# TensorE's order in a two-layer hybrid trunk: one stream at fixed rates, or threads and a rough engine model

## The chip, the cores and the metric

The kernel runs on one core of one Trainium2 chip. The metric is the device time of one execution in microseconds (us); less is better. TensorE (PE in the profile) does the matmuls, VectorE (DVE), ScalarE (ACT) and GpSimd (POOL) the elementwise work, and SyncE (SP) issues the DMA transfers. PEld is TensorE's loading of weights, which runs beside its matmuls.

## The reference

One inference step of a backbone of two layers. 128 context tokens and 512 latent tokens (640 in all) of width 1024 go through the same weights. Each layer normalises and modulates its input, projects it, and gives the columns to three mixers in parallel: A, grouped attention; B, attention over a compressed latent; C, a recurrence over the tokens in both directions. Their outputs are gated, merged and projected.

```python
def _context_mixer(h, lp):
    a_q, a_k, a_v, a_z, b_q, b_ckv, b_kr, b_z, c_in, c_z, gates = _split_in(h @ lp['w_in'])
    q, k, v = _a_qkv(a_q, a_k, a_v, lp)
    ya = _block_attention(q.reshape(...), k, v) * jax.nn.silu(a_z)
    ...
    yb = _mla_attend(qb, ckv, b_kr, lp) * jax.nn.silu(b_z)
    yc, s_f, s_b = _branch_c(c_in, s0, s0, lp)
    yc = yc.astype(h.dtype) * jax.nn.silu(c_z)
    return _merge(gates, ya, yb, yc, lp), k, v, ckv, b_kr, s_f, s_b

# the recurrence of mixer C, for each of 8 heads and both directions
def step(state, inp):
    r_t, w_t, k_t, v_t, a_t, b_t = inp
    sa = jnp.einsum('bhij,bhj->bhi', state, a_t)
    state = (state * w_t[:, :, None, :] + sa[..., None] * b_t[:, :, None, :]
             + v_t[..., None] * k_t[:, :, None, :])
    y_t = jnp.einsum('bhij,bhj->bhi', state, r_t)
    return state, y_t
```

The latent tokens run the same mixers, with rotary positions, and see the cached context as well.

## The kernel before

Activations lie with features on the 128 partitions and the 640 tokens along the row, split into a high and a low part (`hh`, `hl`); each product of full accuracy is three matmuls, high x high, low x high, high x low (L225 to L227 in `proj_half`, L178 to L180 in `mm3`). A tile of 128 output columns is a "unit": `load_w1` brings its weights in two halves (tile `wraw`), ACT casts each to `whi` (L174), DVE or POOL subtracts to get `wlo` (L175), and `proj_half` makes two times 24 matmuls of 320 columns into the PSUM tile `pcm`. Two weight buffers alternate.

Each layer has the stages scan (mixer C, with most projections beside it), attention (mixers A and B), merge and output projection. Only scan and attention are touched.

In the scan stage the heads go in four pairs, p = 0 to 3. For each, `c_prep` makes the decays and the factors `L1` and `BK` (L549 and L551 on DVE, L553 and L554 on POOL), `c_pairs` makes chunk products (`pA`, L613) and transposes, `c_inverse` inverts a triangular matrix by 30 pairs of dependent DVE products (L660, L662) and some small matmuls (`px`, `py`), `c_values` transposes the values. `c_scan` then goes through 2 context and 8 latent chunks, both directions at a time. Each of its 10 steps is a chain over engines: matmul `sca` (L767), copies to `wbd` (L769, L770), matmul `scb` (L773), copies to `VZ` (L775, L776) and, on POOL, to `ubd` (L778), matmul `scb` (L782), matmul `sca` on `ubd` (L786), and the new state on DVE (L799). `c_gn` normalises a pair's output: a chain over POOL, DVE and ACT (L811 to L835), transposes `pyt` (L840), and the last products.

What lies beside a scan is one generator, `self.stream` (the functions `period`, `prepare`, `keys`, `fillers` in `run`): the preparation of the next pair, then units in a fixed order and number from the table `PLAN` (`share`, `fb`, `at`). `pump` takes pieces of it at a fixed rate, three times in each scan step; what is left when the scan ends is run by `drain`. Then come `c_values` of the next pair and `c_gn` of the one that ended. In attention, `stream(i)` holds the next pair's keys and queries, and `head` pumps it at the rates of `PLAN`; `head` makes four tiles of scores (`sc`, L955), each followed by its maximum (L958) and exponential (`P`, L960), then five times transposes (`pp`, L970), the split into `ph` and `pl` (L163, L164), and the two products `po` (L974, L975).

This order of writing is a preference alone: the framework's scheduler then orders the instructions of every engine, TensorE's too, by an own simulation of times, and takes among those that are ready the one written first. On the chip each engine then runs its list in that order.

## Time and profile before

| what | value |
|---|---|
| median of 3 runs | 2347.88 us (2346.89 to 2358.01) |
| the profiled execution's own time | 2358.59 us |
| its span, first to last instruction | 2356.9 us |
| mean granted clock of TensorE | 0.934 |
| busy: PE, PEld | 2144.3 us (91%), 2025.6 us (86%) |
| busy: DVE, ACT, POOL | 1603.2 us (68%), 1107.0 us (47%), 694.8 us (29%) |
| matmuls | 15380 |
| DMA | 209.70 MB, 89 GB/s |

The rows of the trace further below are of the profiled execution. The granted clock is a mean over a stretch: 1.00 is TensorE at 2.4 GHz, 0.50 at 1.2 GHz. A matmul's busy time overlaps that of the next one.

### The profile page before, as it was taken

The numbers are of one execution on the slowest core, as the hardware profiler recorded it, in microseconds if no ns is written. First come the engines' busy times: TensorE is split into PE (matmuls) and PEld (weight loads), VectorE is DVE, ScalarE is ACT, GpSimd is POOL, SyncE is SP. The second block draws the span as 40 slices with busy tenths as digits, with TensorE's granted clock in tenths as the row PEclk, the third lists the DMA queues.
The fourth block names the chain that finished last, engine by engine and source line by source line (L and its number), as shares of the span: only waits on it lengthen the run. The fifth ranks groups of instructions, "written<-read, shape, count | busy, mean of one in ns | idle before, by whom it ended". The sixth has DMA issues, their size and how long they took to land. (4 is left out here: it accounts for less than half of the span.)

```text
span 2356.9 us, 40407 instructions
## 1 busy us (share of the span) xinstructions
PE 2144.3 (91%) x15380; PEld 2025.6 (86%) x15380; DVE 1603.2 (68%) x3054; ACT 1107.0 (47%) x2462; POOL 694.8 (29%) x769
## 2 busy tenths in 40 slices
PE   8889998999779889999989999999897888999998
PEld 6889998989678777879988999989896877788898
DVE  4667878868544677775748778687774458677673
ACT  4544443444343567662344444443442436677333
POOL 3332536145233311102033143351632341210021
PEclk9999998999789899999989999999996989999999
DMA  6232222222223311125622322222222220110552
GB/s 224 77 100 80 82 75 81 86 90 94 79 75 98 107 36 52 39 76 172 203 64 68 106 73 86 74 71 84 81 82 76 73 95 30 51 46 17 186 183 89
DMA packets 111762, 209.70 MB, mean 89 GB/s; under 512 B 14416, under 2 KB 33488, under 8 KB 111568
## 3 DMA queue, kind: packets, MB, share of 16 engines
q1 hardware_dynamic: 111568, 207.12, 27.6%
q8 instruction: 121, 1.98, 0.3%
q14 instruction: 73, 0.60, 0.1%
HBM read 163.52 MB, written 43.55 MB: 88 GB/s over the span
## 5 line engine op out<-in xcount | busy, mean ns | idle before, releaser
L225 PE MATMUL pcm<-hh,whi 128*128 128x320 f32 x1952 | 636.1, 326 | 16.5 <-ACT xv L378 2.9
L227 PE MATMUL pcm<-hh,wlo 128*128 128x320 f32 x1952 | 627.9, 322 | 11.3 <-DVE wlo L175 11.3
L226 PE MATMUL pcm<-hl,whi 128*128 128x320 f32 x1952 | 625.1, 320 | 0.0
L225 PEld LDWEIGHTS pcm<-hh,whi 128*128 128x128 f32 x1952 | 382.1, 196 | 24.5 <-DVE modc L252 5.0
L227 PEld LDWEIGHTS pcm<-hh,wlo 128*128 128x128 f32 x1952 | 380.9, 195 | 15.1 <-DVE wlo L175 13.9
L226 PEld LDWEIGHTS pcm<-hl,whi 128*128 128x128 f32 x1952 | 381.9, 196 | 1.2
L174 ACT CAST whi<-wraw 128x512 fp32r<-128x512 f32 (+1 forms) x356 | 226.9, 666 | 322.0 <-PE pcm L226 116.8
L175 DVE TENSOR_TENSOR wlo<-wraw,whi 128x512 fp32r<-128x512 f32 (+1 forms) x262 | 220.9, 857 | 78.3 <-ACT whi L174 74.9
L175 POOL TENSOR_TENSOR wlo<-wraw,whi 128x512 fp32r<-128x512 f32 x94 | 124.4, 1337 | 157.4 <-ACT whi L174 152.4
L778 POOL COPY ubd<-VZ 64x128 f32<-64x128 f32 x160 | 65.0, 406 | 354.9 <-ACT VZ L775 324.3
L164 DVE TENSOR_TENSOR pl<-pp,ph 128x512 fp32r<-128x512 f32 x160 | 107.9, 684 | 35.5 <-ACT ph L163 34.7
L958 DVE TENSOR_REDUCE nm<-sc 128x1 f32<-128x640 f32 x128 | 104.2, 818 | 28.7 <-PE sc L955 27.5
L178 PE MATMUL pm<-yh,whi 128*128 128x320 f32 x384 | 121.5, 317 | 2.0 <-DVE OT L992 1.5
L179 PE MATMUL pm<-yl,whi 128*128 128x320 f32 x384 | 121.1, 315 | 0.5 <-DVE yl L167 0.4
L180 PE MATMUL pm<-yh,wlo 128*128 128x320 f32 x384 | 120.8, 315 | 0.7 <-DVE wlo L175 0.7
L163 ACT CAST ph<-pp 128x512 fp32r<-128x512 f32 x160 | 92.1, 585 | 46.5 <-PE pp L970 36.6
L960 ACT ACTIVATE P<-sc,nm 128x640 f32<-128x640 f32 x128 | 101.9, 797 | 17.4 <-DVE nm L958 14.0
L970 PE MATMUL pp<-small,P 128*128 128x128 f32 x640 | 102.0, 284 | 7.3 <-DVE pl L164 2.5
L767 PE MATMUL sca<-VZ,L 128*128 128x64 f32 x640 | 96.5, 296 | 11.1 <-DVE VZ L799 11.1
L767 PEld LDWEIGHTS sca<-VZ,L 128*128 128x128 f32 x640 | 93.8, 217 | 12.8 <-DVE VZ L799 12.3
L970 PEld LDWEIGHTS pp<-small,P 128*128 128x128 f32 x640 | 81.9, 146 | 25.0 <-DVE OT L992 3.9
L613 PE MATMUL pA<-L,BK 128*128 128x128 f32 x640 | 93.1, 290 | 6.3 <-DVE BK L549 3.1
(375 smaller groups left out, 4987.5 us busy)
## 6 DMA issues: line engine op xcount, KB each, us to landing
wraw<-in_win SPq DMA_DIRECT2D x156, 256.0 KB, 3.0
wraw<-in_wg SPq DMA_DIRECT2D x96, 256.0 KB, 3.0
wraw<-in_wmod SPq DMA_DIRECT2D x64, 256.0 KB, 3.1
gsp<-gt SPq DMA_DIRECT2D x48, 320.0 KB, 2.6
gt<-gsp SPq DMA_DIRECT2D x48, 320.0 KB, 3.5
wraw<-in_wo SPq DMA_DIRECT2D x24, 512.0 KB, 4.4
cm<-gsl SPq DMA_DIRECT2D x26, 320.0 KB, 2.7
wraw<-in_wmod SPq DMA_DIRECT2D x16, 512.0 KB, 6.6
```

The lines of the kernel that those rows point to most:

```text
L164: self.V.tensor_tensor(out=lo, in0=src, in1=f32(hi), op=ALU.subtract)
L174: self.S.copy(out=hi[part], in_=raw)
L175: sub.tensor_tensor(out=lo[part], in0=raw, in1=f32(hi[part]), op=ALU.subtract)
L178: self.PE.matmul(out, lhsT=lh, rhs=rh, start=first, stop=False)
L179: self.PE.matmul(out, lhsT=lh, rhs=rl, start=False, stop=False)
L180: self.PE.matmul(out, lhsT=ll, rhs=rh, start=False, stop=last)
L225: PE.matmul(p[0:m, 0:H], lhsT=wh[:, kt], rhs=self.hh[:, kt, rs], start=(kt == 0), stop=False)
L226: PE.matmul(p[0:m, 0:H], lhsT=wh[:, kt], rhs=self.hl[:, kt, rs], start=False, stop=False)
L227: PE.matmul(p[0:m, 0:H], lhsT=wl[:, kt], rhs=self.hh[:, kt, rs], start=False, stop=(kt == KT - 1))
L767: PE.matmul(a4[:, d, h], lhsT=L1[h][:, uu[d]].rearrange("p a s -> p (a s)"), rhs=VZ[h][:, cc[d], :], start=(h == 0 and d == 0), stop=False ...
L958: V.tensor_reduce(out=nm, in_=sc[:, :, 0:H], axis=AX.XY, op=ALU.max, negate=True)
L970: PE.transpose(p[:, qt * 128:(qt + 1) * 128], Ps[qt][:, t * 128:(t + 1) * 128], ident)
```

## The change

TensorE's order in the scan and attention stages of each layer is fixed to the order in which the Python program emits it (`tc.manual_schedule` for that engine alone). What is emitted next is decided while the program is written, by a loop over Python threads (generators). A thread yields what its next matmuls need: tiles that have to be written, a PSUM tag that has to be free, another thread's state, or that DVE's backlog is under 1.5 us. `Model` follows every emitted instruction and gives each engine a time by a formula in its size; the loop takes the first thread in order of rank that is ready at TensorE's time, and if none is, the one that is ready first. `PLAN` keeps only an order of the early units.

```diff
 PLAN = [
-    dict(share=[7, 5, 5, 7, 13], fb=[0, 0, 3], at=[3, 2, 1, 0, 2, 1], rate=1.0,
-         early=[38, 29, 19, 20, 21, 26, 37, 23, 28, 18, 30, 31, 34],
-         gates=[1, 0, 0, 0, 0, 1, 1, 0], rates=[8, 8, 22, 30, 21, 16, 25, 13]),
...
+    dict(early=[-1, 38, 29, -2, 19, 20, 21, -3, 26, 37, 23, -4, 28, 18, 30, 31, 34]),
...
+class Model:
...
+    def cost(self, e, inst, n):
+        if e == "act":
+            return 0.14 + 0.92e-3 * n
+        if e == "dve":
+            return 0.12 + 1.3e-3 * n
+        if "pow" in str(getattr(inst, "op", "")):
+            return 2.0
+        return 0.15 + 2.65e-3 * n if "TensorTensor" in type(inst).__name__ else 0.15 + 1.2e-3 * n
...
+            if inst.is_transpose:
+                d = 0.85e-3 * n
+            elif "float32r" in str(ins[0].dtype):
+                d = max(0.06, 0.46e-3 * n)
+            else:
+                d = max(0.224, 1.75e-3 * n)
+            self.pe = max(self.pe, t) + d
+            end = self.pe + 0.3
+        elif e == "sp":
+            end = max(self.pe, t) + (0.0 if on[0][0].startswith("wraw") else 3.0)
...
+class Loop:
+    MARGIN = 0.2
...
+    def run(self, until):
+        while not until():
+            best, tb = None, INF
+            for t in self.threads:
+                a = self.at(t.need)
+                if a <= self.m.pe:
+                    best, tb = t, a
+                    break
+                if a < tb:
+                    best, tb = t, a
...
+            self.m.urgent = best.rank == 0
+            try:
+                with self.tc.high_priority(offset=3000) if best.rank == 0 else ExitStack():
+                    best.need = next(best.gen)
...
+    def free_engine(self):
+        m = self.model
+        return self.V if m.load("dve", m.pe) <= m.load("pool", m.pe) + 0.3 else self.G
...
-            sub.tensor_tensor(out=lo[part], in0=raw, in1=f32(hi[part]), op=ALU.subtract)
+            (sub or self.free_engine()).tensor_tensor(out=lo[part], in0=raw, in1=f32(hi[part]), op=ALU.subtract)
...
+    def dense(self):
+        ahead = None
+        while True:
+            while ahead is None and not self.queue:
+                yield (lambda: len(self.queue) > 0)
+            if ahead is None:
+                ahead = self.queue.pop(0)
+                next(ahead.gen)
+            cur, ahead, self.inunit = ahead, None, True
+            for need in cur.gen:
+                yield need
+                if ahead is None and self.queue:
+                    ahead = self.queue.pop(0)
+                    next(ahead.gen)
...
     def proj_half(self, ps, wh, wl, half):
...
+        yield ["f", wl]
...
-    def c_scan(self, l, e, ps, rate):
+    def c_scan(self, l, e, ps):
...
+                yield [e.VZt, "c"]
...
-                self.pump(rate)
+                yield Wb
...
-                self.pump(rate)
                 if need_z:
+                    yield e.VZt
                     for d in range(2):
                         PE.matmul(cb_[:, 256 + d * 128:384 + d * 128], lhsT=BT[:, uu[d]].rearrange("p h i -> p (h i)"),
                                   rhs=e.VZt[:, :, cc[d], :], start=True, stop=True, skip_group_check=True)
-                self.pump(rate)
-                for d in range(2):
-                    PE.matmul(ca[:, d * 128:d * 128 + 128], lhsT=AB[:, uu[d]].rearrange("p a s -> p (a s)"),
-                              rhs=Ub[:, d].rearrange("p h i -> p (h i)"), start=False, stop=True, skip_group_check=True)
...
+                yield Ub
+                for d in range(2):
+                    PE.matmul(ca[:, d * 128:d * 128 + 128], lhsT=AB[:, uu[d]].rearrange("p a s -> p (a s)"),
+                              rhs=Ub[:, d].rearrange("p h i -> p (h i)"), start=False, stop=True, skip_group_check=True)
...
+    def values(self, e, h, ps):
...
+        late = None
         for t in range(5):
+            yield [*Ps, "pt"]
             p = ps.tile([128, 512], F32, tag="pt", name="pp")
...
             split(ph, pl, p)
-            PE.matmul(po, lhsT=VS[:, 1 + t, :], rhs=ph, start=(t == 0), stop=False)
-            PE.matmul(po, lhsT=VS[:, 1 + t, :], rhs=pl, start=False, stop=(t == 4))
-            self.pump(rate)
+            if late:
+                yield [*late[1:], VS, *(("po",) if po is None else ())]
...
+                product(*late)
+            late = t, ph, pl
+        yield [*late[1:]]
+        product(*late)
...
+    def layer(self, l, ctx_c, ctx_e, wp, st, ps, pool, P):
...
+        def chain():
+            for p in range(4):
+                yield lambda: n.prepared > p
+                e = n.es[p]
+                yield from self.c_values(e, e.xv, ps)
+                n.valued += 1
+                yield from self.c_scan(l, e, ps)
...
+                loop.spawn(norm(e), 1)
+
+        dense = loop.spawn(self.dense(), 4)
+        ch = loop.spawn(chain(), 0)
+        loop.spawn(invert(), 1)
+        loop.spawn(prepare(), 2)
+        loop.run(lambda: n.prepared == 4 and n.normed >= 3)
...
+        at = loop.spawn(self.attention_start(l, pools, wp, st, ps), 3)
+        loop.run(lambda: n.normed == 4 and at.done and all(u.done for u in early) and not self.inunit and self.column is None)
...
+        self.attention(l, at.result, wp, st, ps, lambda: all(u.done for u in queue) and self.column is None)
```

In attention the threads are `values` (rank 0), `scores` (1), `following`, which makes the next pairs' keys and queries (2), and `gates` (3), with the dense queue behind them (4). Yields of the same kind stand ahead of every group of matmuls in `c_prep`, `c_pairs`, `c_inverse`, `c_bonus`, `c_gn` and the attention helpers. `modulation` is split in two, its second matmul being a thread of rank 2. The load of `lnx` moves from `c_prep` to `c_gn`, which takes its PSUM from tag "g" in place of "c". In layer 0 the dense queue holds 4 `z` spills, 13 early units, 24 gates and 24 modulations, and the 12 projections of mixer C are put at its head; in layer 1 there are 8 modulations.

## Rows read from the trace of the kernel before

**Rows 1.** Windows: us, busy (count) of PE, PEld, DVE, ACT, POOL, then PEclk, DMA.

```profile
62.00:794.00 732.00, 657.46 (x5089) 634.79 (x5089) 497.78 (x992) 316.31 (x727) 277.23 (x317) 0.92 0.28 88
794.00:1060.00 266.00, 243.50 (x1513) 211.57 (x1513) 202.61 (x372) 178.70 (x409) 43.25 (x37) 0.96 0.17 53
...
1232.00:1935.00 703.00, 639.70 (x4811) 619.35 (x4809) 492.04 (x977) 298.32 (x685) 247.86 (x295) 0.92 0.25 81
1935.00:2200.00 265.00, 239.70 (x1499) 209.50 (x1500) 195.58 (x356) 174.88 (x402) 36.92 (x33) 0.96 0.16 49
```

**Rows 2.** Windows again: before and after one wait, and a dense stretch.

```profile
646.00:656.00 10.00, 1.47 (x7) 1.47 (x8) 4.31 (x8) 0.74 (x1) 4.10 (x2) 0.50 0.01 3
656.00:667.00 11.00, 9.19 (x41) 8.70 (x40) 7.12 (x17) 4.37 (x11) 3.95 (x9) 0.50 0.16 50
1100.00:1150.00 50.00, 50.00 (x343) 50.00 (x342) 34.77 (x49) 14.29 (x17) 12.06 (x7) 1.00 0.60 186
```

**Rows 3.** Windows within the two scan stages.

```profile
117.00:215.00 98.00, 92.04 (x758) 89.94 (x758) 66.38 (x136) 41.17 (x82) 23.41 (x20) 0.95 0.30 92
...
388.00:546.00 158.00, 148.99 (x1195) 144.99 (x1195) 117.34 (x231) 70.04 (x160) 65.42 (x77) 0.95 0.27 87
546.00:656.00 110.00, 87.66 (x730) 83.43 (x730) 73.67 (x167) 44.52 (x109) 42.14 (x59) 0.84 0.24 76
656.00:747.00 91.00, 82.70 (x583) 79.66 (x582) 40.23 (x109) 39.56 (x101) 26.73 (x46) 0.88 0.27 81
747.00:794.00 47.00, 38.29 (x272) 36.23 (x271) 24.48 (x51) 15.29 (x35) 20.48 (x15) 0.93 0.46 148
1315.00:1380.00 65.00, 64.55 (x569) 63.48 (x567) 46.98 (x113) 27.99 (x56) 4.28 (x7) 1.00 0.31 98
1428.00:1556.00 128.00, 120.98 (x964) 117.87 (x962) 96.75 (x192) 57.67 (x132) 44.50 (x52) 0.96 0.27 86
1556.00:1702.00 146.00, 137.54 (x1073) 134.40 (x1074) 110.44 (x226) 63.70 (x149) 57.89 (x73) 0.93 0.24 78
1702.00:1820.00 118.00, 99.19 (x780) 96.35 (x779) 76.74 (x168) 44.16 (x106) 38.03 (x53) 0.83 0.24 78
1820.00:1911.00 91.00, 82.44 (x548) 79.15 (x546) 44.09 (x117) 37.76 (x96) 31.33 (x48) 0.86 0.25 77
1911.00:1935.00 24.00, 15.66 (x84) 13.37 (x82) 17.07 (x33) 7.94 (x19) 14.42 (x11) 0.83 0.33 106
```

**Rows 4.** TensorE's waits in scan (layer 1 last): us, times, longest.

```profile
PE pyt L840 <- POOL YY L835: 14.8, 2, 13.4
PE scb L773 <- DVE wbd L770: 9.0, 6, 2.7
...
PE sca L767 <- DVE VZ L799: 5.5, 3, 2.6
...
PE pyt L840 <- DVE YY L835: 3.5, 1, 3.5
...
PE pyt L840 <- POOL YY L835: 17.9, 2, 13.2
```

**Rows 5.** Timeline of PE: start, us, instruction, in brackets the wait before.

```profile
654.53 2.40 PE L840 MATMUL pyt<-small,YY 128*128 128x128 f32 x10 [13.38 <-POOL YY L835]
656.72 1.81 PE L767 MATMUL sca<-VZ,L 128*128 128x64 f32 x8
```

**Rows 6.** TensorE's waits in layer 0's attention stage, 794 to 1060 us.

```profile
PE sc L955 <- ACT P L960: 4.4, 12, 0.9
PE po L975 <- DVE pl L164: 3.8, 9, 0.7
```

**Rows 7.** One line's or tile's instructions: ns at least, median, most.

```profile
L551 DVE SCALAR_TENSOR_TENSOR L<-kkn,TP x16: 807/1980/2087, 99.0 to 1668.7; 64x640 f32<-64x640 f32 x16
...
L175 DVE TENSOR_TENSOR wlo<-wraw,whi x108: 651/686/2020, 62.1 to 778.4; 128x512 fp32r<-128x512 f32 x108
L175 POOL TENSOR_TENSOR wlo<-wraw,whi x50: 1263/1286/1868, 96.4 to 792.5; 128x512 fp32r<-128x512 f32 x50
```

648 lines of the change are left out of this document (436 added, 212 removed).

## The prediction

> **What bounds the kernel now.** I read the windows first, cut at the stages: for each stage the time, TensorE's busy time (PE), its weight loads (PEld), DVE, and the granted clock [rows 1]. TensorE is the engine with the least left over everywhere: in layer 0's scan stage (62 to 794 us) it is busy 657.46 of 732 us, DVE 497.78, ACT 316.31, POOL 277.23; the attention stage that follows has 243.50 of 266. Two things are lost there: the time in which TensorE stands, and the time in which the clock is at its lower level of 1.2 GHz. The granted clock is a mean of 1.00 (2.4 GHz) and 0.50, so 732 us at 0.92 hold 673 us at full clock. Lost in layer 0's scan stage: 732 - 657.5 = 74.5 standing and 0.08 x 732 = 58.6 by the clock, 133 in all. Likewise layer 1's scan stage: 63.3 + 56.2 = 119.5. The attention stages by the same count: 22.5 + 10.6 = 33 and 25.3 + 10.6 = 36. Together 322 us out of 1966; nothing else in the program is touched.
>
> That count flatters attention, since busy spans of pipelined matmuls overlap. In the best dense stretch 343 matmuls of 320 columns fill 50 us without a gap, and the weight loads fill it too [rows 2]; in attention the weight loads fill only 211.57 of 266 us and 209.50 of 265 us [rows 1], so by them 54 and 56 us are open. The Trainium skill (Perfetto Trace Analysis, Identifying the Most-Contended Engine) says that matmul busy time is no good measure of distance to the limit and that the share of weight loads is one. By busy time the attention stages hold 69 us to win, by weight loads 110; the trace has both rows and I use the pair as ends.
>
> Next I cut the scan stages into shorter windows [rows 3]. With "lost" as above, the middle of each stage loses 10.9 of 98 us (11%), 16.9 of 158 (11%), 12.1 of 128 (9%), 18.7 of 146 (13%); one stretch, 1315 to 1380, loses 0.5 of 65. The ends are another picture: 39.9 of 110 (36%), 19.2 of 91, 12.0 of 47 in layer 0, and 38.9 of 118 (33%), 21.3 of 91, 12.4 of 24 in layer 1. These six windows are 481 us and lose 143.7 of the 253.
>
> The waits tell why [rows 4]. The longest are those of `pyt`, the transposes at the end of `c_gn`, on the last POOL or DVE operation of that chain: 14.8 + 3.5 us in layer 0 and 17.9 in layer 1. One of them in the timeline [rows 5]: TensorE stands 13.38 us before `pyt`, and the first matmul of the next scan, `sca`, runs right behind it. `sca` needs nothing of `c_gn`: this wait is one of order, not of data. After it the clock is 0.50 until at least 667 us [rows 2], so the stand is paid for again by slow matmuls. The other waits are scan hops (`scb` on `wbd`, `sca` on `VZ`), 9.0 and 5.5 us in layer 0.
>
> **The change part by part.** The arithmetic hardly changes, and the number of matmuls doesn't. TensorE's order inside `layer` becomes the order in which the Python threads emit; the other engines stay with the framework's scheduler, rank 0 being moved forward there. (A) *No order waits at the ends.* `c_gn` becomes a thread of its own, the scan has rank 0, and all dense units (12 projections, 4 `z`, 13 early, 24 gates, 24 modulations in layer 0; 8 modulations in layer 1) form one queue of the lowest rank, so there is work beside every wait as long as the queue lasts, and what is left of it moves on into attention instead of being forced into the last period. The six end windows hold 481 - 143.7 = 337 us of work; at the 11% that well-filled windows lose they take 337 / 0.89 = 379: -102 us. Bounds: only the three `pyt` sums go, 36 us, with half as much again of slow clock: -54; or the ends become like 1315 to 1380: -141.
>
> (B) *The middle windows.* The rest of the scan stages is 954 us with 109 lost. There dense chunks of six matmuls (0.88 us at 50 / 343 = 0.146 us each) now stand between the hops of a scan step, placed where the operand isn't there yet, and the second state product goes ahead of the one that waits for POOL's `ubd`. Bounds: 0, because these windows already had filler, and -102, as in 1315 to 1380. I take a third of the loss, -36, since the stretches without any loss had no scan or preparation at its expensive point.
>
> (C) *Attention.* `values` multiplies one tile later than it transposes, so `pl` of one tile is made beside the transposes of the next; `scores` is a thread of its own; dense units fill. The named waits are small, 4.4 us for `sc` on `P` and 3.8 for `po` on `pl` in layer 0 [rows 6]; DVE is busy 202.61 of 266 us, so attention can't go under some 205. Bounds 0 and -75 for both layers, I take -40: between the 69 and the 110 us a little under half.
>
> (D) *What is handed back.* The threads' clock prices a DVE operation of 640 elements at 0.12 + 0.0013 x 640 = 0.95 us. In the trace the products of `c_prep` at L551 take 0.81 at best and 1.98 at the median [rows 7]; they run beside POOL's products on the same operands, which stay where they are. Four for each direction are 8 in a preparation, so DVE is up to 8 us later than the threads believe, and the first `pA` stands in TensorE's order with all behind it. I charge half, 4 us, for each of 8 preparations: +33; bounds 0 and +66. The same clock has the `wlo` subtraction on DVE at 0.79 against 0.69 in the trace, and on POOL at 1.51 against 1.29 [rows 7]; those are on the safe side. Nothing is charged for the moved `lnx` load and `z` spills: they are issued from SP far ahead of their use, beside DMA that is 0.28 busy [rows 1]; if that cover went, one load of weights would be late by its own transfer, within the bounds of (B).
>
> Sum: -102 - 36 - 40 + 33 = -145 us on the profiled execution's 2358.59 us: 2213.6. The median of the runs is 2347.88, 0.45% below that execution, so I scale by 0.9955: 2204 us.
>
> **The rivals.** *Full cover (2115 us).* All scan windows lose 5% (work 599 + 583 in 630 + 614 us, -191), attention gives its -60, little is handed back: -250, scaled 2099; with 15 us for the start and end of the stages 2115. For it speaks 1315 to 1380; against it that no window with a running scan came near that.
>
> *DVE or the scan's own chain paces the stage (2274 us).* Dense work runs out before the fourth scan ends, as it does now; then only the order waits go (-54) and half of attention's gain (-20): 2284.6, scaled 2274. For it speaks DVE at 498 of 732 us, with 60 dependent products of an inverse in each preparation; if the stage shrinks to 640, DVE is at 78% of it. `free_engine` pushes that both ways: it sends `wlo` halves to POOL when DVE is behind. The Trainium skill (SBUF — State Buffer, Who interferes with whom) says that a DVE instruction with two SBUF inputs contends with a GpSimd instruction that reads SBUF, and that the loser is blocked. The rows at L551, and the 2.02 us maximum of a `wlo` that takes 0.69 [rows 7], agree; by that rule unloading DVE onto POOL gives it less than it takes, and the time would be this rival's. Against it: TensorE alone has 599 us of work in that stage, 101 more than DVE.
>
> *Slower (2394 us): TensorE's fixed order meets engines that don't keep it.* Place: every point at which a thread hands over, some 1,120 of them by the diff (four in each of 80 scan steps, some 35 in each of 8 preparations, some 260 in each attention stage). DVE, ACT and POOL are still ordered by a scheduler that doesn't know the threads' clock; an eviction that it puts behind a 2 us product holds up the matmul that waits for it and, now, all dense work behind. A + B + C are 178 us, so the point from which it decides is 178 / 1120 = 0.16 us more at a hand-over than planned, on average; at 0.20 us it is 224 - 178 = +46, 2404.6, scaled 2394. Against it: a margin of 0.2 us is added to every forecast, dense matmuls are 0.146 us in the trace and 0.147 in the threads' clock.
>
> *Nothing moves (2348 us).* The scheduler could already take any ready matmul first, and one set of wrong timings takes the place of another. Against it: the 36 us of `pyt`.
>
> **How the numbers follow.** The measurement tells about 0.5% from no change. Chances: forecast 0.48, full cover 0.15, DVE or chain 0.20, nothing 0.05, slower 0.12. Faster by over 0.5%: 0.48 + 0.15 + 0.20 = 0.83; same 0.05; slower 0.12. The forecast is the likeliest single case, 2204 us. The range goes from full cover, 2115, past the DVE rival to 2300 (B at 0 and D at +66 on top of the forecast: 2213.6 + 36 + 33 = 2283, scaled 2272, and a little of A); outside lie the slower case, nothing, and the edge of full cover, 0.2.
>
> **What would show it.** A: no `pyt` wait of several us, no window of the scan stage under 0.90 of clock. B: mean clock in the scan stages above 0.95, and less than 45 us standing in each. C: weight loads above 85% of the attention stage. D: the longest remaining waits are `pA` on DVE. DVE rival: long stretches without `pcm` late in the scan stage, or `pcm` all gone before attention. Slower: more time standing than the 74.5 and 63.3 us of now, in many waits of 0.3 to 1 us on DVE and ACT. I am wrong if the scan stage keeps its length while TensorE's work in it is the same.

## The result and the profile after

The changed kernel takes 2554.38 us (median of 4 runs, 2552.28 to 2559.0) against 2351.16 us of the kernel before beside it: ratio 1.0864, 95% interval 1.083 to 1.0898. The forecast was 2204 us, with a range to 2300; it is wrong, and on the wrong side. The span is 2552.3 us against 2356.9, 195 us more.

First the page of the kernel after, busy time by engine (share of the span, count):

```profile
PE 2199.8 (86%) x15380; PEld 2071.3 (81%) x15380; DVE 1613.2 (63%) x2950; ACT 1114.8 (44%) x2462; POOL 830.3 (33%) x873
```

The same 15380 matmuls, a busy time that is 2.6% up, and no other engine near its limit. So the 195 us are standing time and low clock. Windows by stage (columns as in [rows 1]; the last is a piece of attention that is read further below):

```profile
62.00:800.00 738.00, 627.90 (x4711) 603.82 (x4710) 498.15 (x922) 300.47 (x688) 318.00 (x350) 0.90 0.24 76
800.00:1197.00 397.00, 319.89 (x1896) 283.36 (x1897) 217.41 (x400) 198.71 (x451) 59.55 (x50) 0.88 0.17 55
1370.00:2067.00 697.00, 625.79 (x4748) 605.38 (x4749) 482.02 (x896) 294.71 (x673) 318.61 (x345) 0.94 0.24 79
2067.00:2398.00 331.00, 266.46 (x1568) 232.38 (x1569) 204.24 (x382) 183.83 (x417) 42.66 (x37) 0.89 0.14 45
...
1097.00:1134.00 37.00, 24.93 (x121) 22.12 (x121) 14.43 (x38) 12.30 (x26) 5.76 (x5) 0.68 0.24 83
```

Against [rows 1]: the scan stages are 738 and 697 us long (732 and 703), attention 397 and 331 (266 and 265). All of the loss, 131 + 66 us, is in attention. But the scan stage of layer 0 didn't stay as it was either: 378 fewer matmuls ran in it (4711 for 5089), and it is 6 us longer. They went to attention, which has 383 more: 288 dense ones, which are six units, and 90 short ones (`pmod`) of five modulations. At 0.146 us for the first and 0.06 us for the second (the 16 `pmod` from 1118.13 us, below, start within 0.9 us) that is 47 us of work.

The clock: 2 x (1 - 0.88) x 397 = 95 us of layer 0's attention, and 73 us of layer 1's, were at 1.2 GHz; by [rows 1] it was 21 in each.

What ends TensorE's waits in the scan stages (us, times, longest), layer 0 and then layer 1:

```profile
PE scb L1021 <- DVE wbd L1018: 28.7, 12, 8.2
PE scb L1030 <- DVE VZ L1024: 22.6, 10, 4.2
...
PE pyt L1095 <- DVE L L1086: 6.2, 1, 6.2
...
PE scb L1030 <- DVE VZ L1024: 15.7, 8, 3.7
PE scb L1021 <- DVE wbd L1018: 12.6, 10, 2.0
...
PE pyt L1095 <- DVE L L1086: 4.2, 1, 4.2
```

Of the kernel before, layer 0, one line beside those of [rows 4]:

```profile
PE scb L782 <- DVE VZ L776: 2.9, 5, 0.8
```

`pyt`, 18.3 us in layer 0 before, is down to 6.2. In its place stand the scan's own hops: `scb` on `wbd` 28.7 us where it was 9.0 [rows 4], and the second `scb`, on `VZ`, 22.6 where it was 2.9. One of them in the timeline (start, us, engine, line):

```profile
395.43 1.00 PE L1015 MATMUL sca<-VZ,L 128*128 128x64 f32 x8
...
396.47 0.26 ACT L1017 COPY wbd<-sca 64x128 f32<-64x128 f32 x1 [0.85 <-PE sca L1015]
396.80 2.07 DVE L772 SCALAR_TENSOR_TENSOR ta<-ta,kkn 128x640 f32<-128x640 f32 x1
...
398.80 4.01 DVE L785 SCALAR_TENSOR_TENSOR L<-kkn,TP 64x640 f32<-64x640 f32 x2
...
402.84 2.60 DVE L782 SCALAR_TENSOR_TENSOR BK<-ta,TM 64x640 f32<-64x640 f32 x2
405.47 0.28 DVE L1018 COPY wbd<-sca 64x128 f32<-64x128 f32 x1
...
405.81 1.22 PE L1021 MATMUL scb<-wbd,AB 128*128 128x128 f32 x4 [6.62 <-DVE wbd L1018]
```

`wbd` is written in halves. ACT has done its half at 396.73; DVE's half is behind five products of the next pair's preparation and runs at 405.47. TensorE stands 6.62 us: the rival "Slower", as it was described.

In attention no single wait is long. In layer 0 the longest sums are these:

```profile
PE poc L1203 <- DVE OT L1170: 9.6, 8, 1.9
PE pqr L1434 <- DVE QR L1441: 7.5, 2, 4.8
```

The way between two pairs of heads tells more. TensorE from the last `po` of one pair to the first scores of the next, with a line of ACT and one of DVE:

```profile
1097.26 0.44 PE L1236 MATMUL po<-pl,VS 128*128 128x512 f32 x1
...
1102.40 0.63 PE L1434 MATMUL pqr<-small,qr 128*64 128x128 f32 x4 [0.53 <-ACT gt L1572]
1107.84 0.39 PE L1434 MATMUL pqr<-small,qr 128*64 128x128 f32 x1 [4.81 <-DVE QR L1441]
1110.16 0.61 PE L426 MATMUL pcm<-hh,whi 128*128 128x320 f32 x1 [1.93 <-DVE QR L1441]
...
1117.64 0.44 ACT L1572 ACTIVATE gt<-pcm 128x320 f32<-128x320 f32 x1
1118.13 0.22 PE L450 MATMUL pmod<-whi,sc_t 128*4 128x128 f32 x1 [1.58 <-ACT gt L1572]
...
1119.60 0.47 PE L358 MATMUL pvb<-uv,KB 128*128 128x128 f32 x1 [0.34 <-ACT mrow L452]
1123.07 0.69 DVE L339 TENSOR_TENSOR VS<-pvb,VS 128x512 fp32r<-128x512 f32 x1 [13.06 <-ACT VS L338]
1126.74 0.67 PE L358 MATMUL pkh<-KB,uk 128*128 128x384 f32 x1
...
1133.72 0.36 PE L1219 MATMUL sc<-KH,QT 128*128 128x320 f32 x1
```

For 34 us, until the next pair's first context scores (`scc`, at 1131.87, just ahead of the last line), no head's scores or values are worked on. The next pair's queries (`pqr`), values (`pvb`) and keys (`pkh`) are made one after another, each waiting for its eviction. A piece of a dense unit (`pcm`, from 1110.16) doesn't lie beside this chain but in it: `pvb` comes behind, and DVE is idle for 13.06 us until `VS`. The clock of the 37 us window is 0.68. In the kernel before, the same steps were pieces of `stream(i)` and lay beside the heads of the pair ahead.

### The profile page after: what moved, and what is told of

Same layout as the page of the kernel before. It is cut to its first block, busy times and chain, and to the rows that moved or that the text cites. A ratio compares the mean times of both kernels' runs of the same rounds, so it can differ in the third digit from the quotient of the medians.

```text
span 2552.3 us, 40302 instructions
## 1 busy us (share of the span) xinstructions
PE 2199.8 (86%) x15380; PEld 2071.3 (81%) x15380; DVE 1613.2 (63%) x2950; ACT 1114.8 (44%) x2462; POOL 830.3 (33%) x873
## 3 DMA queue, kind: packets, MB, share of 16 engines
q8 instruction: 121, 1.98, 0.3%
## 4 chain that ended last, share of the span: by engine, by line
PE 32%; DVE 11%; ACT 5%; issue 4%; POOL 2%; DMA 2%; SPq 0%; DVEq 0%; ACTq 0%; POOLq 0%
PE pcm L426 4%; PE pcm L427 3%; PE pcm L428 3%; PE pm L358 2%; PE pm L360 2%; PE pm L359 2%; PE sc L1219 2%; DVE LN L905 1%; DVE NF L903 1%; PE pout L358 1%; PE pout L360 1%; PE pout L359 1%; PE pA L850 1%; PE pp L1243 1%; POOL wlo L355 1%
## 5 line engine op out<-in xcount | busy, mean ns | idle before, releaser
L426 PE MATMUL pcm<-hh,whi 128*128 128x320 f32 x1952 | 668.3, 342 | 48.8 <-DVE gsl L642 8.6
L427 PE MATMUL pcm<-hl,whi 128*128 128x320 f32 x1952 | 634.3, 325 | 0.0
L426 PEld LDWEIGHTS pcm<-hh,whi 128*128 128x128 f32 x1952 | 398.6, 204 | 60.7 <-ACT xr L585 10.1
L355 POOL TENSOR_TENSOR wlo<-wraw,whi 128x512 fp32r<-128x512 f32 x203 | 276.5, 1375 | 469.7 <-ACT whi L354 452.1
L428 PEld LDWEIGHTS pcm<-hh,wlo 128*128 128x128 f32 x1952 | 394.8, 202 | 8.7 <-POOL wlo L355 8.1
L427 PEld LDWEIGHTS pcm<-hl,whi 128*128 128x128 f32 x1952 | 397.6, 204 | 1.8 <-issue 0.2
L355 DVE TENSOR_TENSOR wlo<-wraw,whi 128x512 fp32r<-128x512 f32 (+1 forms) x153 | 156.8, 1034 | 86.1 <-ACT whi L354 82.9
L905 DVE TENSOR_TENSOR LN<-LN,NF 128x30 f32<-128x30 f32 (+14 forms) x240 | 106.0, 442 | 6.5
L903 DVE TENSOR_TENSOR NF<-LN 128x30 f32<-128x30 f32 (+14 forms) x240 | 105.6, 440 | 6.3
L1021 PE MATMUL scb<-wbd,AB 128*128 128x128 f32 x320 | 54.4, 294 | 41.4 <-DVE wbd L1018 41.3
```

The lines of the kernel that those rows point to most:

```text
L355: (sub or self.free_engine()).tensor_tensor(out=lo[part], in0=raw, in1=f32(hi[part]), op=ALU.subtract)
L426: PE.matmul(p[0:m, 0:H], lhsT=wh[:, kt], rhs=self.hh[:, kt, rs], start=(kt == 0), stop=False)
L427: PE.matmul(p[0:m, 0:H], lhsT=wh[:, kt], rhs=self.hl[:, kt, rs], start=False, stop=False)
L428: PE.matmul(p[0:m, 0:H], lhsT=wl[:, kt], rhs=self.hh[:, kt, rs], start=False, stop=(kt == KT - 1))
L903: V.tensor_tensor(out=pv_, in0=LNv[:, s + 1:32, s:s + 1].to_broadcast([128, m, s]), in1=LNv[:, s:s + 1, 0:s].to_broadcast([128, m, s]), op ...
L905: V.tensor_tensor(out=LNv[:, s + 1:32, 0:s], in0=LNv[:, s + 1:32, 0:s], in1=pv_, op=ALU.add)
```

## The experiments

The stage lengths below are read from the trace of each run: scan from the last `plo` to the first context scores `scc`, attention from there to the last `pri`. In brackets stands the number of dense units (48 `pcm` matmuls) that started in the stage.

| kernel | median us | ratio (95%) | scan 0 | attention 0 | scan 1 | attention 1 |
|---|---|---|---|---|---|---|
| before | 2351.16 | | 733 (54) | 266 (8) | 702 (54) | 267 (8) |
| after | 2554.38 | 1.0864 (1.083-1.0898) | 738 (48) | 397 (14) | 697 (53) | 331 (9) |
| e1, order free | 2491.73 | 1.0585 (1.0534-1.0636) | 744 (48) | 336 (14) | 730 (53) | 294 (8) |
| e7, free in attention | 2488.08 | 1.0599 (1.0566-1.0632) | 738 (48) | 346 (14) | 703 (53) | 309 (9) |
| e2, no priority | 2555.0 | 1.0863 (1.0797-1.093) | 737 (48) | 398 (14) | 696 (53) | 330 (9) |
| e3, margin 1.0 | 2532.18 | 1.0766 (1.07-1.0833) | 743 (52) | 342 (10) | 727 (53) | 327 (9) |
| e4, `wlo` as before | 2544.36 | 1.0818 (1.0752-1.0884) | 700 (44) | 409 (18) | 703 (53) | 330 (9) |
| e5, no hold | 2639.6 | 1.1223 (1.118-1.1266) | 710 (41) | 428 (18) | 671 (44) | 403 (18) |
| e6, all early | 2530.1 | 1.0769 (1.0731-1.0808) | 742 (49) | 357 (13) | 747 (57) | 285 (5) |
| e9, all early, queue empty | 2568.61 | 1.0958 (1.0917-1.0999) | 832 (61) | 280 (1) | 778 (61) | 282 (1) |
| e8, all early, free in attention | 2479.32 | 1.0545 (1.0523-1.0567) | 742 (49) | 310 (12) | 752 (57) | 263 (5) |
| e10, products on DVE | 2541.11 | 1.0814 (1.0771-1.0857) | 720 (47) | 402 (15) | 686 (53) | 329 (9) |
| b1, norm beside | 2312.32 | 0.9839 (0.9801-0.9876) | 708 (54) | 266 (8) | 676 (53) | 269 (9) |
| b2, values late | 2352.97 | 1.0013 (0.9991-1.0035) | 730 (54) | 261 (8) | 699 (54) | 270 (8) |
| b4, five units to attention | 2364.57 | 1.0054 (1.003-1.0078) | 717 (49) | 298 (13) | 700 (54) | 266 (8) |
| b3, b1 and products on DVE | 2291.18 | 0.9754 (0.9718-0.979) | 705 (54) | 266 (8) | 654 (53) | 265 (9) |

A ratio is to runs of the kernel before on the same chip.

### Is it the fixed order? e1 and e7

e1 is the changed kernel without the fixed order:

```diff
-                with tc.manual_schedule(engines={mybir.EngineType.PE}):
+                with ExitStack():
                     self.layer(l, ctx_c, ctx_e, wp, st, ps, pool, P)
```

> One edit: TensorE's order in the scan and attention stages is left to the framework's scheduler again; what the threads emit, and in which order, stays. Theory H (hand-overs: a fixed order of TensorE meets engines that are ordered by another clock): most of the 200 us go, 2350 to 2430, and the waits of scb on wbd (28.7 us in layer 0's scan stage) fall under 10. Theory P (pairs in a row: the threads' conditions leave too little beside the chain of an attention pair, whoever orders TensorE): attention keeps 380 and 320 us and the time stays above 2500.

e7 keeps it in the scan stage:

```diff
+                self.man = ExitStack()
+                self.man.enter_context(tc.manual_schedule(engines={mybir.EngineType.PE}))
                 self.layer(l, ctx_c, ctx_e, wp, st, ps, pool, P)
...
         ps = P(f"psB{l}", f=1, pt=2, po=1, S=2)
+        self.man.close()
         self.attention(...)
```

> The changed kernel with TensorE's order fixed in the scan stages alone; in attention the scheduler orders TensorE again. With the order free in both (2492 us) attention was 61 and 37 us shorter, and the scan stages 6 and 33 us longer. Theory 'the fixed order costs its time in attention alone and is worth something in the scan': both attention stages shrink as they did there (397 to about 336, 331 to about 294) and the scan stages stay at 738 and 697: 2455 to 2470 us. Theory 'what attention won there it won because the scan took longer and left it less': scan stages as in the changed kernel, attention shrinks by less than half of that, 2510 to 2550 us.

Windows of e7's attention stages:

```profile
803.00:1148.00 345.00, 300.19 (x1892) 267.53 (x1891) 212.88 (x400) 196.01 (x450) 59.17 (x50) 0.95 0.20 64
...
2025.00:2334.00 309.00, 261.90 (x1565) 228.03 (x1563) 204.50 (x382) 181.20 (x417) 44.69 (x37) 0.91 0.15 48
```

The same matmuls (1892 and 1565), 52 and 22 us less, and a higher clock. e1 and e7 end at the same time, so fixing the order in the scan stages too changes nothing in the end (e1's scan stages are 6 and 27 us longer than e7's, its attention 10 and 15 us shorter). In attention the fixed order costs 66 us. That is a third of the loss. e1 fits neither of its theories: it gains far less than the first wanted and more than the second allowed; e7 lies between its two. The hops of the scan wait with a free order too (e1, layer 0's scan stage):

```profile
PE scb L1021 <- DVE wbd L1018: 17.4, 11, 3.8
PE scb L1030 <- DVE VZ L1024: 10.9, 9, 3.9
```

28.3 us in place of 51.3, but still over twice as long as before (9.0 on `wbd` [rows 4], and 2.9 on `VZ`), and the stage is no shorter, though TensorE's order is free.

### Three settings of the threads: e2, e3, e4

e2 leaves out the priority of rank 0 on the other engines:

```diff
-                with self.tc.high_priority(offset=3000) if best.rank == 0 else ExitStack():
+                with ExitStack():
```

> One edit: instructions of rank 0 are no longer moved forward for the framework's scheduler. H: the scan's evictions queue later still on DVE and ACT, scb's waits grow, 2570 to 2650. If the moved priority itself spoils the order of the other engines: 2450 to 2530. P: attention is as long as before this edit within 15 us, the change is in the scan stages alone.

No difference, which neither range of times allowed: this setting does nothing here. e3 raises the margin on every forecast:

```diff
-    MARGIN = 0.2
+    MARGIN = 1.0
```

> One edit: every forecast of an operand gets a margin of 1.0 us in place of 0.2, so more dense matmuls go in ahead of each hand-over. H: late operands are covered, 2500 to 2530, fewer waits of scb, less time at the lower clock. P: chains get longer and nothing fills them in attention: 2555 to 2600, the loss being in attention.

22 us less, 2 us above the range of the first theory, and not in the scan: there stage 1 is 30 us longer with the same 53 units. Four units more ran in layer 0's scan stage, for 5 us, and attention without them is 55 us shorter. e4 puts the low halves `wlo` on the engines of before:

```diff
...
-                self.sub = None
+                self.sub = self.V
```

> One edit: wlo is subtracted where it was before the change (DVE for the scan stage's units, POOL for the modulation's and in attention) in place of on the engine that the threads take to be free. If POOL's 203 wlo (94 before the change) slow DVE's products with two inputs: the inverse's products fall from 440 ns back to some 360 and the time to 2480 to 2530. H and P both: 2540 to 2600, since DVE has more to do in the scan stage.

Four units fewer fit in layer 0's scan stage, which is 38 us shorter, and go to attention: 10 us less in all, with an interval that overlaps that of the changed kernel. The products of the inverse do what the expectation said: 349 ns on average before, 441 in the changed kernel with 203 `wlo` on GpSimd, 367 here with 114. The time doesn't follow. So none of these settings is the main cause; what shows in e3 and e4 is that units wander between the stages.

### Does the preparation pace the scan? e5

```diff
-        D1 = ("load", "dve", 1.5)
+        D1 = ("load", "dve", 1e9)
...
```

The same line is changed in `c_prep`, `c_inverse` and `c_gn`.

> The changed kernel with the hold on the preparation taken off: in the program as written, VectorE's work for the next pair may be put down however far VectorE's own clock in the model has run ahead (it was held back at 1.5 us). Everything else is as in the changed kernel (2554 us). Theory 'the preparation paces the scan stage' (in the changed kernel the first normalisation product of a pair and its first inverse product lie 68 us apart, in the kernel before 28, and the scan of the next pair stands until they are done): those 68 us fall to 30 to 45, the two scan stages (738 and 697 us) shorten by 20 to 60 us together, and the time is 2480 to 2530 us. Theory 'the fixed order meets engines that keep another' : VectorE's own backlog grows, and the scan's evictions queue behind more of it; scan stages no shorter or longer, 2550 to 2600 us. Theory 'only attention lost the time': scan stages within 10 us, 2545 to 2565 us.

```profile
62.00:772.00 710.00, 583.38 (x4300) 558.36 (x4299) 494.42 (x910) 280.70 (x649) 305.46 (x340) 0.86 0.21 68
```

From the first normalisation product (`pn2`) to the first `pA` the four preparations of layer 0 take 29, 29, 45 and 56 us before, 47, 68, 65 and 62 after, and 38, 59, 52 and 66 here: the hold explains some of it, not most. Both scan stages are shorter, by 28 and 26 us. The trace shows what each scan waits for: the last matmuls `py` of its own pair's inverse. The second pair of layer 0, before and then after:

```profile
328.86 3.91 PE L693 MATMUL py<-AB,LN 32*32 32x32 f32 x80
...
366.67 1.81 PE L767 MATMUL sca<-VZ,L 128*128 128x64 f32 x8
```

```profile
372.66 2.41 PE L940 MATMUL py<-AB,LN 32*32 32x32 f32 x80
...
378.03 1.00 PE L1015 MATMUL sca<-VZ,L 128*128 128x64 f32 x8
```

In the changed kernel all eight scans start 2.9 to 5.5 us after that; before, the inverses of the second to fourth pairs were done 30 to 50 us ahead. The scans themselves are shorter now: 97, 92 and 83 us from the first to the last `sca` in layer 0, in place of 141, 115 and 107. From the first `pn2` to the last `py` the four preparations with their inverses take 546 us in layer 0 and 541 in layer 1 before, 601 and 580 after. The stages follow this chain: against the changed kernel it is 25 and 36 us shorter here (the stages 28 and 26), 17 and 12 shorter in e10 (18 and 11), 9 and 48 longer in e6 (4 and 50); in e3 and e4 chain and stage lie up to 16 us apart. So the preparation of the pairs, with the inverse, paces the scan stages of the changed kernel. In e5's first scan stage 7 units fewer ran too, 49 us; b4, below, gets back half of what it takes out, so what these units alone are worth of the 28 us can't be told apart. The work went into attention, and the whole is 85 us longer, beyond every expectation. A scan stage that ends sooner sends its dense work to a worse place.

### What does a unit cost in attention? e6, e9, b4

e6 asks for all of attention's projections ahead of it, by longer `early` lists; e9, further, doesn't begin attention before the dense queue is empty:

```diff
-        loop.run(lambda: n.normed == 4 and at.done and all(u.done for u in early) and ...
+        loop.run(lambda: n.normed == 4 and at.done and all(u.done for u in early + queue) and ...
```

> The changed kernel with every projection that was still planned inside attention asked for ahead of it, so that none of attention's chains waits for one; the arithmetic is the same. Theory 'attention's pairs run one after another with too few threads to fill the gaps': attention loses the dense work that filled it, which goes into the scan stage; the scan stages grow by 20 to 50 us, attention shrinks by 20 to 50 us, time 2540 to 2580 us. Theory 'attention waits for its own projections' (the evictions of query and value projections stand between two pairs' scores, 36 us from the last values product of one pair to the first scores of the next at 1097 to 1134 us): attention of layer 0 shrinks from 397 us by 60 to 120, that of layer 1 from 331 by 30 to 60, scan stages grow by at most 30 together; 2430 to 2500 us.

> The changed kernel with every projection asked for ahead of attention (2530 us by itself) and, further, attention not begun before the whole dense queue is done: no dense unit is left for attention. The 13 units that lay in layer 0's attention there and the 5 in layer 1's, 7 us each at full clock, go to the scan stages' ends: these grow to some 835 and 782 us. Theory 'a unit moved into attention costs at least its full time there, since nothing of it is hidden' : a pair of heads without a unit takes 27 to 35 us as now, attention is 240 to 260 us in each layer (from 357 and 285), and the whole 2500 to 2535 us, no worse than with the units in attention. Theory 'units in attention are hidden in its gaps': attention stays above 300 and 270 us, and the time is 2560 to 2620 us.

Attention of e6, then of e9:

```profile
804.00:1161.00 357.00, 300.09 (x1875) 270.29 (x1875) 205.60 (x382) 195.70 (x447) 59.05 (x50) 0.91 0.19 60
...
2086.00:2371.00 285.00, 237.13 (x1394) 200.96 (x1393) 197.17 (x368) 177.27 (x406) 37.02 (x32) 0.92 0.18 58
```

```profile
894.00:1174.00 280.00, 215.51 (x1181) 175.61 (x1182) 192.76 (x362) 168.82 (x385) 28.75 (x25) 0.88 0.14 45
...
2124.00:2406.00 282.00, 219.68 (x1182) 181.08 (x1183) 193.22 (x362) 169.08 (x385) 28.72 (x25) 0.85 0.15 46
```

e6: with the projections there, layer 0's attention is 40 us shorter with nearly the same matmuls (1875 for 1896). Layer 1's is 46 us shorter; four units of it, 28 us, went to its scan stage, which is 50 us longer. So asking late costs, but more than half of what is won is given back in layer 1's scan stage; the time lies between the two ranges. e9: with nearly no dense work attention still takes 280 and 282 us, more than the 266 and 265 of before with eight units. So TensorE's work doesn't set its length; the chain over the engines from pair to pair does, and that chain got longer. Put back at the scan stages' ends the units cost 90 us for the 12 units and seven modulations (92 us at 0.146 and 0.06 us a matmul) that layer 0's stage has more than in e6: behind the scans a unit costs its full time too. The time, 2568.61 us, is in the second theory's range, but only half by its reason: layer 0's attention did fall under its 300, to 280; layer 1's stayed above its 270, at 282.

b4 does the opposite in the kernel before: six gate units are taken out of layer 0's scan stage as written and put beside the first six pairs, at the fixed rates; by the counts, five moved:

```diff
-    dict(share=[7, 5, 5, 7, 13], ...
-         gates=[1, 0, 0, 0, 0, 1, 1, 0], rates=[8, 8, 22, 30, 21, 16, 25, 13]),
+    dict(share=[7, 5, 5, 7, 7], ...
+         gates=[1, 1, 1, 1, 1, 1, 0, 0], rates=[16, 16, 30, 38, 29, 24, 25, 13]),
```

> The kernel before with six gate units of layer 0 moved from its scan stage into attention, one beside each of the first six pairs of heads, at the fixed rates (raised by eight steps a pair for them). It is the amount that the change moves there (264 us of TensorE's work in place of 215, here about 257), with the old way of placing it. Theory 'a unit in attention costs its time, whoever places it': attention of layer 0 grows from 266 by 40 us or more, the scan stage loses 30 to 42 us, the time is 2345 to 2365 us. Theory 'fixed rates hide it, the threads don't': attention grows by 10 to 25 us, the scan stage loses as much or more, 2325 to 2350 us, no slower than before.

```profile
62.00:779.00 717.00, 631.26 (x4858) 606.78 (x4858) 500.82 (x999) 310.88 (x713) 286.60 (x321) 0.90 0.27 83
779.00:1077.00 298.00, 273.83 (x1749) 244.42 (x1747) 194.00 (x353) 185.63 (x426) 52.17 (x45) 0.97 0.19 62
```

By the matmul counts (5089 and 1513 before), 231 left the scan stage, 34 us of work, and gave back 15 us. 236 came to attention, 34 us, and cost 32. This is the first theory but for two sizes (40 us or more in attention, 30 to 42 in the scan): a unit more costs its time in attention under the old placing too, and the scan stage gives back half.

### Do the two causes in attention add up? e8

e8 is e6 and e7 together.

> The changed kernel with both repairs of attention: every projection asked for ahead of it (2530 us by itself, attention 357 and 285 us) and TensorE's order free in attention (2488 us by itself, 346 and 309 us). Theory 'two causes that add up': attention falls to about 310 and 265 us, 2455 to 2475 us. Theory 'one and the same wait, of dense matmuls that stand in the fixed order behind an operand that was asked for late': the second repair gives little on top of the first, attention stays at 335 to 350 and 280 to 290 us, 2500 to 2525 us.

```profile
808.00:1117.00 309.00, 274.68 (x1802) 246.19 (x1801) 202.01 (x380) 190.19 (x442) 56.91 (x49) 0.96 0.21 67
...
2059.00:2323.00 264.00, 230.71 (x1401) 192.63 (x1399) 198.94 (x369) 175.29 (x405) 37.17 (x32) 0.95 0.20 62
```

In attention they add up: it takes 309 and 264 us, as expected for that, and its clock is back at 0.96 and 0.95. Of the 88 and 67 us to the changed kernel, 13 and 27 are two and four units that ran elsewhere, less one modulation each that came in; 75 and 40 are the order and the late asking. Layer 0's stage has four units and six modulations (34 us) more than before; at their full price that is 266 + 34 = 300, 9 us under the measured. The time is 2479.32, above the expected 2455 to 2475, since layer 1's scan stage is 752 us long. It isn't held up at its end (from the last `scb` to `scc` 21 us, 22 in the changed kernel); its preparations take longer, 630 us from the first `pn2` to the last `py` where the changed kernel has 580.

Pair by pair (us from the last `po` of one pair to that of the next, the first from its `scc`; units started in brackets), layer 0:

| kernel | 1 | 2 | 3 | 4 | 5 | 6 | 7 | 8 |
|---|---|---|---|---|---|---|---|---|
| before | 35 (1) | 37 (1) | 32 (1.4) | 32 (1.6) | 38 (1) | 33 (1) | 36 (1) | 23 (0) |
| after | 35 (0) | 54 (2) | 63 (3.4) | 31 (1.6) | 72 (2.9) | 42 (2.1) | 72 (2) | 27 (0) |
| e9 | 35 (0) | 38 (0) | 47 (1) | 26 (0) | 34 (0) | 34 (0) | 35 (0) | 31 (0) |
| e8 | 32 (0) | 32 (1) | 39 (2.5) | 36 (1.5) | 41 (1.5) | 47 (2) | 45 (1.5) | 38 (2) |

Most pairs take some 31 to 38 us by their own chain, with no unit (e9) or with one (before). One unit is about free there, and before had just that. After has two and three in some pairs and none in others, and a pair with two or more takes 42 to 72; in e8 it takes 38 to 47.

### Single parts of the change on the kernel before: b1, b2

b1 puts `c_gn` of a pair at the head of the stream beside the next pair's scan, with its PSUM from tag "g". For that the sum of both directions is taken first, intermediate results go to other tiles, and the pump rate of a scan rises by the pieces that came in; all else stays:

```diff
+                    if prev:
+                        yield from self.c_gn(prev, ps)
                     z = self.spill(self.silu2, l, W_CZ + p, wp, st, ps, self.zsp[p])
...
-                    self.c_gn(prev, ps)
+                self.play(self.c_gn(prev, ps))
```

> The kernel before (2352 us here) with one part of the change alone: the group norm, gate and transposition of a pair's y go into the stream beside the next pair's scan and no longer stand in TensorE's order at the end of their own scan; the transposition's PSUM is the stream's. The rates stay. Theory of the forecast's first term (every pair's end costs a wait of TensorE of about 13 us and a stretch at a lower clock behind it, some 100 us over eight pairs, of which six have a next scan to lie beside): 2265 to 2310 us. Theory 'the scan's end is paced by the preparation of the next pair, which goes on meanwhile': the wait moves to another name at the next pair's start, 2335 to 2365 us. Slower, over 2365 us, if VectorE's and ScalarE's work for the group norm comes in the way of the next scan's evictions.

```profile
61.00:769.00 708.00, 654.67 (x5091) 634.19 (x5092) 493.29 (x995) 317.50 (x728) 283.01 (x317) 0.93 0.29 90
...
1205.00:1881.00 676.00, 626.44 (x4758) 606.31 (x4757) 481.20 (x960) 291.26 (x673) 241.03 (x291) 0.93 0.25 81
```

Faster by 36 us, just short of the 2265 to 2310 expected. All waits of `pyt` in the whole run come to 1.1 us, and TensorE is busy 654.67 us of a stage that is 24 us shorter than before. The preparations (`pn2` to `pA`) are all at 29 to 33 us. The mechanism is right; its size is that of the waits themselves, 36 us.

b2 multiplies with the values one tile later:

```diff
...
-            PE.matmul(po, lhsT=VS[:, 1 + t, :], rhs=ph, start=(t == 0), stop=False)
-            PE.matmul(po, lhsT=VS[:, 1 + t, :], rhs=pl, start=False, stop=(t == 4))
+            if late:
+                product(*late)
+            late = t, ph, pl
             self.pump(rate)
+        product(*late)
```

> The kernel before with another part of the change alone: in attention the product of the probabilities with the values is put one tile later in TensorE's order, behind the next tile's scores and its dense work. Theory of the forecast's third term (TensorE stands at these products for the eviction of the probabilities, 3.8 to 4.4 us each in the longest, and more of it at a lower clock behind): attention's 266 and 267 us shrink by 10 to 25 us each, 2300 to 2335 us. Theory 'ScalarE's exponentials and the split of the probabilities pace a head': the wait moves to the scores or to the last product, 2345 to 2360 us.

```profile
PE sc L955 <- ACT P L960: 4.4, 11, 0.7
PE po L970 <- DVE pl L164: 3.5, 8, 0.6
```

Nothing, as its second theory said. Even the wait that it was made for stays, 3.5 us for 3.8 [rows 6]. The traces of both kernels show why: transposes `pp` of a later tile and products `po` already alternate before, and nearly the same order comes out here, since the scheduler orders TensorE again. So b2 moved almost nothing.

### The products that share their operands: e10, b3

In both kernels the 64 products of 64x640 that GpSimd makes go to DVE:

```diff
-                G.tensor_tensor(out=BK[r_, us, 1 - h, :], in0=v3(kd, h), in1=tB[r_, :, oB:oB + 64], op=ALU.mult)
-                G.tensor_tensor(out=L1[h][r_, us, 1, :], in0=v3(xr, h), in1=tR[r_, :, oR:oR + 64], op=ALU.mult)
+                V.tensor_tensor(out=BK[r_, us, 1 - h, :], in0=v3(kd, h), in1=tB[r_, :, oB:oB + 64], op=ALU.mult)
+                V.tensor_tensor(out=L1[h][r_, us, 1, :], in0=v3(xr, h), in1=tR[r_, :, oR:oR + 64], op=ALU.mult)
```

> The changed kernel with the 64 products of 64x640 that GpSimd makes beside VectorE's on the same operands moved to VectorE. VectorE's 64 products take 1.66 us on average there (0.81 at best); alone all 128 should take 0.81 each, 104 us in place of 106, and GpSimd loses some 118 us of work. Theory 'the scan's evictions stand behind VectorE products of 2 us': with products of 0.81 us TensorE's waits for wbd and VZ (28.7 and 22.6 us in layer 0's scan stage) fall by a third or more and the time by 15 to 40 us, 2515 to 2540 us. Theory 'the products are not the cause': 2545 to 2570 us. Slower, over 2570 us, if VectorE's products stay at 2 us alone and double its load.

> The kernel before with the group norm beside the next scan (2312 us by itself) and GpSimd's 64 products of 64x640 moved to VectorE too, where they should take 0.81 us each without GpSimd on the same operands. If VectorE's time stays the same and its pieces get shorter, the preparation of a pair loses some 4 to 8 us of GpSimd's work and the time is 2285 to 2310 us; if VectorE's products don't get shorter, VectorE gains 50 to 100 us and the time is 2330 to 2380 us.

One of DVE's old products (ns at least, median, most) in b1, where GpSimd runs beside it, and in b3:

```profile
L553 DVE SCALAR_TENSOR_TENSOR L<-kkn,TP x16: 806/1984/2120, 98.3 to 1673.8; 64x640 f32<-64x640 f32 x16
```

```profile
L553 DVE SCALAR_TENSOR_TENSOR L<-kkn,TP x16: 806/820/823, 99.0 to 1645.2; 64x640 f32<-64x640 f32 x16
```

1984 ns become 820. The 128 products of b3 take 118.0 us of DVE, the 64 of b1 104.6; DVE's busy time for the whole kernel is 1572.6 us in b3 and 1589.1 in b1. So GpSimd's half costs DVE 13 us. b3 is at 0.9754 of before, b1 at 0.9839: some 20 us, by the ratios. It is the fastest of all, 2291.18 us, faster than both kernels and in its expected range.

In the changed kernel it gives 13 us, less than the least that was expected of the eviction theory, and the intervals of the two overlap. Two rows of layer 0's scan stage, two of layer 1's:

```profile
PE scb L1030 <- DVE VZ L1024: 21.8, 11, 3.7
...
PE scb L1021 <- DVE wbd L1018: 12.3, 10, 4.5
...
PE scb L1021 <- DVE wbd L1018: 21.7, 9, 5.7
PE scb L1030 <- DVE VZ L1024: 14.0, 10, 2.7
```

The four sums are 69.8 us against 79.6. Layer 0's fell, layer 1's rose. So the 2 us products are at most a part of the hops' wait, seen in the timeline above.

## Why the prediction was wrong

**The step that failed is the first one.** The prediction read TensorE's standing time and low clock as time that work can fill, and made A, B and C shares of it. b4 shows that it can't be read so: 34 us of matmuls out of the scan stage shorten it by 15, and e9 shows an attention of 280 us with almost nothing dense in it. Chains over the engines set attention's length and, in the changed kernel, that of the scan stages, where each scan starts right behind the inverse of its pair; TensorE's dense work lies beside them. TensorE busy for 90% didn't show that, and the weight loads, the stricter measure, didn't either. "I am wrong if the scan stage keeps its length while TensorE's work in it is the same" came about, and more: 738 us with 47 us less work. By b4's measure these 47 us should have made it 21 shorter; it is 6 longer, so some 27 us were lost there.

**A, -102 us.** The mechanism was right: in the changed kernel `pyt` waits only 6.2 and 4.9 us in the two scan stages, and in b1 it is gone. The size was not. The part by itself is worth 36 us, the sum of the waits; the other loss of the six end windows was no order wait. It was predicted at a level that well-filled windows reach, and b1's scan stages keep the clock at 0.93.

**B, -36 us, bounds 0 and -102.** The scans of the second to fourth pairs did get shorter, from 363 to 272 us in layer 0 and from 344 to 250 in layer 1, but the stages didn't: each scan now waits for its inverse. And TensorE stands more, 110 and 71 us where it was 74.5 and 63.3. The two `scb` hops alone wait 51.3 us in layer 0's scan stage and 28.3 in layer 1's; before, 11.9 in layer 0. The bound at nothing rested on filler that was there already; it left out that a faster scan meets the preparation of the next pair on DVE.

**C, -40 us, bounds 0 and -75.** This is the term that decided: +197. Its own mechanism, values one tile late, was there already in the scheduler's order (b2). What it left out are three prices. Work that the scan stage sends there: 47 us of matmuls in layer 0 and one unit, 7 us, in layer 1, at the full price that b4 measures. The fixed order, 52 and 22 us by itself (e7), and projections asked for only when the threads get there: the two together 75 and 40 us (e8). That is 122 of the 131 us in layer 0, and 47 of the 66 in layer 1. A (the queue "moves on into attention instead of being forced into the last period") named the first and took it for a gain.

**D, +33 us.** Right that the preparations get later, wrong in where it is paid and too small. TensorE waits 1.9 us in all for `pA` in layer 0; it is the scans that wait, behind a chain of preparations and inverses that is 55 us longer in layer 0 and 39 in layer 1, together over the bound of 66. The long products were charged as the reason; with most of them at 0.82 us the changed kernel gains 13 us (e10).

**The rivals.** "Slower" named a mechanism that is there: DVE puts an eviction behind products, TensorE and all its dense work wait. But its place is wrong. It was spread over 1,120 hand-overs, more than half of them in the scan stages; there, freeing the order changes nothing in the end (e1 against e7). In attention, 66 us over some 520 hand-overs are 0.13 us each, under the 0.16 from which it was to decide. Nor did it make the sign: with TensorE's order free the kernel is still slower than before, at 1.0585 (e1). "DVE or the scan's own chain paces the stage" was right in its title, for attention and for the changed kernel's scan stages, where the inverse that it names is the last part of the chain. Its time, 2274, was wrong, since it kept half of attention's gain and took the dense work that a chain leaves no place for as free.

**What stays open.** What makes the preparations longer. From `pn2` to `pA` the four of layer 0 take 242 us together, 159 before; the hold is 27 of that (e5), the priority of rank 0 is nothing (e2). Why the hops of the scan wait over twice as long as before even when the scheduler orders TensorE (28.3 us in e1); the product length explains a part at most. And 9 of the 131 us of layer 0's attention and 19 of the 66 of layer 1's. An order of DVE made by the threads' own clock wasn't tried.

## What to carry to other kernels

Before reading standing time as room, move a known piece of work out of the stage, as b4 does: if the stage gives back less than the piece, a chain paces at least a part of it, and better order on the fullest engine wins less than its standing time. Then look in the trace for what each step starts right behind: here it was the inverse of the next pair. A queue that "moves on" into the next stage is a cost, not a saving, when that stage can hide one unit per step and no more. A fixed order of one engine cost 66 us where a pair's operands come one after another from other engines. A wait found in the timeline was worth about its own length in b1, and nothing in b2: take that length as the most, and move that one step alone.

## What the runs showed of the hardware

A product of two SBUF operands on DVE takes 0.82 us alone and 1.98 us at the median while GpSimd makes another one beside it, and GpSimd needs 1.8 to 1.9 us for its own; 128 of them on DVE alone take 118.0 us of its time, 64 in the shared way 104.6 (b3 and b1). The Trainium skill (SBUF — State Buffer, Who interferes with whom) says that such instructions contend and one is blocked; these rows agree, and here the sharing saved DVE 13 us and cost the kernel some 20. The products of the inverse go the same way: 349 ns on average before, where GpSimd has 94 `wlo` subtractions, 441 in the changed kernel, where it has 203, and 367 in e4 with 114.

The clock followed the gaps. Attention with the same matmuls ran at 0.88 with the order fixed and 0.95 with it free in layer 0, and the 37 us between two pairs of heads, where TensorE stood a third of the time, at 0.68. In the dense unit that lies in this stretch, matmuls follow each other at 0.146 us in its first half (1097.5 to 1101.6, clock 1.00) and, behind the waits for `pqr`, at 0.267 from 1110.16 to 1115.9 (clock 0.50): here a chain that left TensorE waiting was paid for again in the dense work that followed.
